# A two-layer float32 decoder step on one core: decode's retention update split in two and moved partly into the out and gate phases, Strassen over all 16 K tiles in the heads

## The chip, the core and the metric

The kernel runs on one core of a Trainium2 chip. The metric is the device time of one execution in microseconds (us); a kernel is timed several times and the median counts. Beside the times there is the profile of one execution, taken by the hardware profiler. TensorE (PE in the profile) multiplies matrices, VectorE (DVE) and ScalarE (ACT) work element by element on 128 partitions, GpSimd (POOL) here mostly issues transfers, and SyncE (SP) issues the loads of weights.

## What is computed

One inference step of a decoder trunk with two layers, for a prompt of 512 positions and 8 sample rows (one new token each), all in float32. The model width is 2048. Per layer:

```
h = rmsnorm(x, norm_g)
z = h @ w_in                      # 2048 x 8192: b, c, xc, g_conv (1024 each) and q, k, v, g_ret (4 heads of 256)
y_conv = b * conv3(c * xc) * silu(g_conv)
q, k = rope(q), rope(k) / 16
# retention, per head with decay gamma_h:
#   prompt: o_n = sum over m <= n of gamma^(n-m) (q_n . k_m) v_m, in chunks; the final state is an output
#   sample: S_new = gamma * S + k v^T ;  o = q . S_new ;  S_new is an output
y_ret = groupnorm(o) * gn_g * silu(g_ret)
x = x + concat(y_conv, y_ret) @ w_out
x = x + sigmoid(x @ w_pg) * (p[i] @ w_ple)
```

After both layers a final rmsnorm follows. The sample part of the retention is called decode below: 4 heads x 8 rows = 32 states of 256 x 256 numbers per layer, 256 KB each, that are read from DRAM, decayed, increased by an outer product, reduced against the query and written back.

## The kernel before

**Tiling.** Activations are kept transposed: a K tile is 128 model columns (partitions) by 520 columns, the 512 prompt positions and the 8 sample rows. A weight matrix has 16 K tiles, and output tiles of 128 columns are made in pairs (`pair`, line 396). Every float32 product is made of three float32r matmuls on high and low parts (`mm3`, lines 247 to 249): hi x hi, hi x lo, lo x hi. The 520 columns are worked on as two halves of 260, so each matmul has 260 columns. Weights come by SP into a ring `raw` of 32 tiles of 128 columns; `split_w` (lines 229 and 230) makes the high part on ScalarE and the low part on VectorE, into a ring of 60 such tiles that TensorE reads.

**Strassen.** `strassen` (line 290) handles the first s of the 16 K tiles of a pair as a 2 x 2 block product, with the K tiles in two groups, the two output tiles and the two column halves. It makes 7 products instead of 8, each over s/2 tiles. For that it adds and subtracts weight blocks on VectorE (`add`, line 319; four times s/2 tiles) and uses sums of operands prepared once per stage (`operand_sums`, lines 413 to 416, split by lines 551 and 552). The K tiles from s to 15 that are left over go through plain products afterwards, which need a fourth PSUM bank and one copy more. `plain` does a pair without Strassen. How many K tiles go through Strassen is written out by pair in the lists `HEADS`, `CONVS`, `OUT_ROWS` and `GATES` (0 means plain); the host packs the weights' K tiles in the order that each entry needs (`k_order`).

**Stages of a layer.** (1) The heads: for each of 4 heads four pairs make q, k, v and the gate; rope, then the parts are stored to DRAM (`hs`), and nine later steps per head do the prompt's chunked retention. (2) The convolutions: two pairs for each of 8 column tiles. (3) The out phase: 8 pairs with w_out, plus the residual (line 1139), stored as `x1s`. (4) The gate phase: 8 pairs with w_pg, the sigmoid and the embedding product, stored as `x2s`. The last layer ends with a tail of its own in place of the last gate pair. In layer 0 the first two pairs of the heads are done in a preamble.

**Decode before.** `sample_load` (lines 769 and 770) loads a state and, by a broadcast to 128 partitions, its key and query from DRAM (`kq`). `sample_step` scales the state by gamma on ScalarE (line 776), adds key times value on VectorE (line 780, twice 256 columns), stores the state (line 781) and reduces it against the query on VectorE (line 784, twice, each a main instruction and a short one that reads the accumulator). `sample` does one step and one load; it is called after each head pair and in the middle of every second one, and once or twice per column tile of the convolutions. At the last column tile, what is left is finished and `sample_norm` normalises the sums (matmuls of line 1371 against a constant).

**Order of the work.** The Tile framework orders each engine's instructions by priority and by a simulation of its own; `keep` holds marked instructions in program order among themselves. Two lists of callbacks interleave side work: `middle` is emptied after the fifth of a Strassen pair's seven products (or at half of a plain pair), and one entry of `later` is run after the fourth product and one at the end of each pair (in a plain pair right after `middle`, and at its end). Small loads and stores all go through GpSimd's queue (`SIDE`), in order. Tiles live in 75 slots, given out in the order in which they came free; operands of the next stage are built ahead (`fill`) only when enough slots are free.

## Times and profile before

| | |
|---|---|
| device time, median of 3 runs | 2169.59 us (2166.01 to 2169.92) |
| the profiled execution, first to last instruction | 2167.3 us (no other time is given for it) |
| TensorE matmuls | 17861 records, busy 99% of the span |
| VectorE, ScalarE, GpSimd busy | 87%, 58%, 20% |
| mean granted TensorE clock | 0.999 of full speed |
| DMA | 387 MB, mean 179 GB/s |

The median lies 2.3 us above the profiled span. Stages in the profiled execution, by the lines that run: layer 0 heads and convolutions to about 725 us, out phase to about 897, gate phase to about 1105; layer 1 heads and convolutions to about 1790, out phase to about 1970, gate phase and tail to the end. How to read the rows: "L230 DVE" is line 230 of the kernel on VectorE; "out<-in" are the program's own names; "x1031" is a count; after the bar stand busy us, the mean ns of one instruction, and the engine's idle time just before, with what ended it. Matmuls overlap, so a busy TensorE can still be short of matmuls: their number in a stretch tells.

### The profile page before, as it was taken

The numbers are of one execution on the slowest core, as the hardware profiler recorded it, in microseconds if no ns is written. First come the engines' busy times: TensorE is split into PE (matmuls) and PEld (weight loads), VectorE is DVE, ScalarE is ACT, GpSimd is POOL, SyncE is SP. The second block draws the span as 40 slices with busy tenths as digits, with TensorE's granted clock in tenths as the row PEclk, the third lists the DMA queues.
The fourth block names the chain that finished last, engine by engine and source line by source line (L and its number), as shares of the span: only waits on it lengthen the run. The fifth ranks groups of instructions, "written<-read, shape, count | busy, mean of one in ns | idle before, by whom it ended". The sixth has DMA issues, their size and how long they took to land. (4 is left out here: it accounts for less than half of the span.)

```text
span 2167.3 us, 48178 instructions
## 1 busy us (share of the span) xinstructions
PE 2147.8 (99%) x17861; PEld 2142.1 (99%) x17861; DVE 1896.1 (87%) x3849; ACT 1264.5 (58%) x2647; POOL 430.6 (20%) x746
## 2 busy tenths in 40 slices
PE   9999999999999999999999999999999999999998
PEld 9999999999999999999999999999999999999998
DVE  8889988998999987987997988989999998879884
ACT  8656655565555655655765655565645555456565
POOL 2313222211001211200212222231111022011011
PEclk9999999999999999999999999999999999999999
DMA  8555565545543745645645566664464355566455
GB/s 288 171 175 197 181 217 184 178 157 175 158 129 118 238 156 187 215 154 160 215 144 175 172 213 191 189 209 170 151 182 149 120 158 202 176 207 200 128 164 198
DMA packets 182861, 387.31 MB, mean 179 GB/s; under 512 B 25888, under 2 KB 56352, under 8 KB 182624
## 3 DMA queue, kind: packets, MB, share of 16 engines
q1 hardware_dynamic: 128704, 212.98, 31.6%
q0 software_dynamic: 53056, 169.84, 23.8%
q8 instruction: 140, 2.29, 0.4%
q10 hardware_dynamic: 864, 1.39, 0.2%
q14 instruction: 97, 0.79, 0.1%
HBM read 318.96 MB, written 65.15 MB: 177 GB/s over the span
## 5 line engine op out<-in xcount | busy, mean ns | idle before, releaser
L247 PE MATMUL ps_g<-slot,split 128*128 128x260 f32 x5465 | 1531.6, 284 | 7.2 <-ACT slot L307 2.9
L248 PE MATMUL ps_g<-slot,split 128*128 128x260 f32 x5465 | 1534.3, 282 | 0.3 <-DVE slot L555 0.3
L249 PE MATMUL ps_g<-slot,split 128*128 128x260 f32 x5461 | 1519.9, 283 | 0.5 <-DVE split L230 0.5
L229 ACT ACTIVATE split<-raw 128x512 fp32r<-128x512 f32 (+2 forms) x1347 | 777.3, 596 | 583.1 <-DVE raw L319 213.2
L247 PEld LDWEIGHTS ps_g<-slot,split 128*128 128x128 f32 x5465 | 1024.0, 188 | 10.1 <-ACT slot L307 3.7
L248 PEld LDWEIGHTS ps_g<-slot,split 128*128 128x128 f32 x5465 | 1028.5, 188 | 0.5 <-DVE slot L555 0.5
L249 PEld LDWEIGHTS ps_g<-slot,split 128*128 128x128 f32 x5461 | 1019.8, 188 | 1.0 <-DVE split L230 1.0
L230 DVE TENSOR_TENSOR split<-raw,split 128x512 fp32r<-128x512 f32 (+2 forms) x1346 | 849.2, 652 | 172.5 <-PE ps_g L248 85.4
L319 DVE TENSOR_TENSOR raw<-raw 128x512 f32<-128x512 f32 (+1 forms) x660 | 428.9, 660 | 32.5 <-DMA raw<-wi 23.7
L307 ACT ACTIVATE slot<-ps_g 128x260 f32<-128x260 f32 x336 | 127.4, 381 | 140.6 <-PE ps_g L249 122.7
L551 ACT ACTIVATE slot<-slot 128x520 fp32r<-128x520 f32 (+1 forms) x212 | 109.2, 562 | 46.6 <-DVE slot L414 11.1
L552 DVE TENSOR_TENSOR slot<-slot,slot 128x520 fp32r<-128x520 f32 (+1 forms) x212 | 124.4, 620 | 4.1 <-ACT slot L551 3.9
L781 POOL DMA_DIRECT2D o_rets<-slot x64 | 35.3, 552 | 351.6 <-DVE slot L780 131.7
L307 DVE TENSOR_TENSOR slot<-ps_g,slot 128x260 f32<-128x260 f32 x168 | 70.9, 424 | 6.0 <-PE ps_g L249 3.7
L869 POOL DMA_DIRECT2D slot<-hs x64 | 46.2, 724 | 118.7 <-DVE split L230 42.7
L814 POOL DMA_DIRECT2D hs<-slot x64 | 35.6, 556 | 139.3 <-DVE slot L755 61.3
L780 DVE SCALAR_TENSOR_TENSOR slot<-slot,vs,slot 128x256 f32<-128x256 f32 x128 | 56.1, 481 | 4.5 <-ACT slot L776 4.3
L746 DVE TENSOR_TENSOR slot<-slot,slot 128x520 f32<-128x520 f32 x80 | 55.8, 698 | 4.7 <-DMA o_rets<-slot 3.7
L770 POOL DMA_DIRECT2D slot<-sret x64 | 35.5, 554 | 114.6 <-ACT split L229 37.3
L1058 POOL DMA_DIRECT2D slot<-x1s x76 | 40.8, 538 | 87.6 <-PE ps_g L249 27.2
L1209 POOL DMA_DIRECT2D x2s<-slot x30 | 16.4, 545 | 201.6 <-DVE slot L1204 200.6
L771 POOL DMA_DIRECT2D slot<-kq x64 | 34.9, 547 | 106.0 <-DVE slot L876 22.2
(217 smaller groups left out, 1733.8 us busy)
## 6 DMA issues: line engine op xcount, KB each, us to landing
raw<-wi SPq DMA_DIRECT2D x377, 256.0 KB, 3.9
raw<-wo SPq DMA_DIRECT2D x128, 256.0 KB, 5.4
raw<-wg SPq DMA_DIRECT2D x122, 256.0 KB, 4.1
raw<-wi SPq DMA_DIRECT2D x136, 192.0 KB, 4.0
slot<-x1s POOLq DMA_DIRECT2D x76, 260.0 KB, 5.1
slot<-sret POOLq DMA_DIRECT2D x64, 256.0 KB, 4.0
hs<-slot POOLq DMA_DIRECT2D x64, 256.0 KB, 4.0
slot<-hs POOLq DMA_DIRECT2D x64, 256.0 KB, 5.2
```

The costliest lines, as they stand in the source:

```text
L229: S.activation(hi, raw, AF.Copy)
L230: V.tensor_tensor(lo, raw, F(hi), SUB)
L247: PE.matmul(out, wh, xh, start=start, stop=False, skip_group_check=more)
L248: PE.matmul(out, wh, xl, start=False, stop=False, skip_group_check=more)
L249: PE.matmul(out, wl, xh, start=False, stop=stop, skip_group_check=more)
L307: fn(*args)
L319: V.tensor_tensor(out[:, n], x[:, n], y[:, n], op)
L551: keep(S.activation(hi, src[:, n], AF.Copy))
L552: V.tensor_tensor(lo, src[:, n], F(hi), SUB)
L746: V.tensor_tensor(out[:, n], v, table[:, n], MUL)
L780: keep(V.scalar_tensor_tensor(st[:, c], k, vs[:, h, e, b : b + 1], st[:, c], MUL, ADD))
L869: SIDE.dma_start(t[:, :512].rearrange("p (m n) -> p m n", m=2), src)
```

## The change

The lists ask for 16 K tiles where they asked for 14, in the heads and in the first two convolution pairs (the last convolution pair stays at 14). Decode is taken apart. In the heads and convolutions, each state is loaded and reduced against the query with gamma as the factor, without the new key and value; the part of the new key and value in the output, gamma * (q . k/gamma) * v, is worked out for all states at once in `sample_norm` (two matmuls with ones, four small VectorE operations). The queries of two rows come in one broadcast load. The states themselves are updated in the out and gate phases by a chain of three callbacks, each one `update` call apart: `key_load` broadcasts the key, `state_add` makes key times value/gamma on ScalarE and adds the old state to it by an accumulating load from DRAM, `state_out` scales by gamma on ScalarE and stores. One call of `update` does one step of each of three states. It is called in the middle of each out and gate pair, after each, and once more in every second out pair. The vector with gamma is replaced by immediate numbers.

```diff
-HEADS = [[0, 0, 0, 8] + [14] * 12, [0] + [14] * 15]
-CONVS = [[14] * 2 + [16] * 13 + [14]] * 2
+GAMMA = [1.0 - 2.0 ** (-5 - h) for h in range(H)]
+HEADS = [[0, 0, 0, 8] + [16] * 12, [0] + [16] * 15]
+CONVS = [[16] * 15 + [14]] * 2
...
         def sample_load(h, b):
-            st, kb = get(), get()
+            st = get()
             SIDE.dma_start(st[:, :512], sret[l, h, b])
-            SIDE.dma_start(kb[:, :512], kq[l, h, b].rearrange("c d -> (c d)").partition_broadcast(P))
-            return h, b, st, kb
-
-        def sample_step(h, b, st, kb):
-
-            keep(S.activation(st[:, :512], st[:, :512], AF.Identity, scale=gam(h)))
-            k = kb[:, 256:512]
+            if b % 2 == 0:
+                queries.append(get())
+                src = kq[l, h, b : b + 2, :2].rearrange("b c d -> b (c d)").partition_broadcast(P)
+                SIDE.dma_start(queries[-1][:, :512].rearrange("p (b c) -> p b c", b=2), src)
+            return h, b, st, queries[-1]
+
+        def sample_step(h, b, st, q):
+
             for e in range(2):
                 c = slice(256 * e, 256 * e + 256)
-                keep(V.scalar_tensor_tensor(st[:, c], k, vs[:, h, e, b : b + 1], st[:, c], MUL, ADD))
-            SIDE.dma_start(o_rets[l, h, b], st[:, :512])
-            for e in range(2):
-                c = slice(256 * e, 256 * e + 256)
-                V.tensor_tensor_reduce(k, st[:, c], kb[:, :256], 1.0, 0.0, MUL, ADD, osum[:, e, h, b : b + 1])
-            put(st, kb)
+                n = slice(256 * (b % 2), 256 * (b % 2) + 256)
+                keep(V.tensor_tensor_reduce(st[:, c], st[:, c], q[:, n], GAMMA[h], 0.0, MUL, ADD, osum[:, e, h, b : b + 1]))
+            put(st)
+            if b % 2:
+                put(q)
...
+        def key_load(h, b):
+            st = get()
+            SIDE.dma_start(st[:, 256:512], kq[l, h, b, 2:].rearrange("c d -> (c d)").partition_broadcast(P))
+            return h, b, st
+
+        def state_add(h, b, st):
+            for e in range(2):
+                c = slice(256 * e, 256 * e + 256)
+                keep(S.activation(st[:, c], st[:, 256:512], AF.Copy, scale=vs[:, h, e, b : b + 1]))
+            SIDE.dma_start(st[:, :512], sret[l, h, b], accum_op=ADD)
+            return h, b, st
+
+        def state_out(h, b, st):
+            keep(S.activation(st[:, :512], st[:, :512], AF.Copy, scale=GAMMA[h]))
+            SIDE.dma_start(o_rets[l, h, b], st[:, :512])
+            put(st)
+
+        keyed, added = [], []
+
+        def update():
+
+            if added:
+                state_out(*added.pop(0))
+            if keyed:
+                added.append(state_add(*keyed.pop(0)))
+            if states:
+                keyed.append(key_load(*states.pop(0)))
+
+        states = [(h, b) for h in range(H) for b in range(NS)]
...
+            V.scalar_tensor_tensor(qk[:, :, h], qks[:, :2, :NS], GAMMA[h], qks[:, 2:, :NS], MUL, MUL)
...
-                V.scalar_tensor_tensor(vs[:, h, e, :], t[:, SEQ:T], 1.0 / 16, rb[:, SEQ:T], MUL, MUL)
+                V.scalar_tensor_tensor(vs[:, h, e, :], t[:, SEQ:T], 1.0 / 16 / GAMMA[h], rb[:, SEQ:T], MUL, MUL)
...
             Gt.ready = m // 2
             middle.append(lambda: O.fill(MORE_OUT, 0))
+            middle.append(update)
+            if m % 4:
+                later.append(update)
             zs = pair(O, wo[l], m, m // 2, Gt)
+            update()
...
             middle.append(lambda: Gt.fill(MORE_GATE, 0))
+            middle.append(update)
...
             Gt.fill(MORE_GATE, 0)
+            update()
             Gt.need(m // 2 + 1)
...
+    ps = pr.tile([P, 512], F32, tag="r", name="ps_qk")
+    for d in range(2):
+        PE.matmul(ps[:, :n], ones, qk[:, d].rearrange("p h b -> p (h b)"), start=d == 0, stop=d == 1)
+    own = small.tile([P, 2, H, NS], F32, tag="sq", name="own", bufs=1)
+    for e in range(2):
+        V.tensor_tensor(own[:, e], vs[:, :, e], ps[:, :n].rearrange("p (h b) -> p h b", b=NS), MUL)
+        V.tensor_tensor(osum[:, e], osum[:, e], own[:, e], ADD)
```

14 lines of the change are left out of this document (7 added, 7 removed).

## The prediction

> **What bounds the kernel now.** I read the page first, then who TensorE waits for, then the engines' busy time in stretches cut where one stage gives way to the next.
>
> ```profile
> span 2167.3 us, 48178 instructions
> PE 2147.8 (99%) x17861; PEld 2142.1 (99%) x17861; DVE 1896.1 (87%) x3849; ACT 1264.5 (58%) x2647; POOL 430.6 (20%) x746
> ```
>
> ```profile
> PE ps_g L247 <- ACT slot L307: 2.9, 4, 1.3
> PE ps_g L247 <- ACT ps_g L307: 1.6, 2, 1.2
> PE ps_g L247 <- ACT split L229: 1.5, 2, 1.3
> ```
>
> The second fence is the list of waits of TensorE, longest first (us in total, times, longest). Nobody holds TensorE for more than 3 us in 2167. The next view gives us and instructions per engine in a stretch, in the order PE, weight loads, DVE, ACT, POOL, then granted clock, DMA share and GB/s.
>
> ```profile
> 300.00:350.00 50.00, 50.00 (x420) 50.00 (x419) 47.27 (x104) 27.83 (x62) 14.01 (x26) 1.00 0.65 210
> 700.00:735.00 35.00, 31.68 (x260) 31.07 (x260) 35.00 (x75) 26.51 (x71) 10.66 (x20) 1.00 0.80 268
> 735.00:830.00 95.00, 95.00 (x794) 94.98 (x793) 79.59 (x141) 47.49 (x93) 14.04 (x27) 1.00 0.51 162
> 830.00:890.00 60.00, 60.00 (x503) 60.00 (x502) 49.37 (x92) 35.79 (x72) 14.39 (x27) 1.00 0.71 234
> 890.00:915.00 25.00, 25.00 (x211) 25.00 (x210) 24.80 (x54) 13.81 (x26) 4.86 (x9) 1.00 0.57 184
> 1105.00:1480.00 375.00, 373.93 (x3119) 372.74 (x3118) 331.45 (x725) 218.37 (x488) 94.79 (x164) 1.00 0.59 182
> 1770.00:1800.00 30.00, 28.15 (x233) 27.72 (x232) 29.66 (x65) 23.10 (x64) 10.14 (x19) 1.00 0.83 287
> 1965.00:1990.00 25.00, 25.00 (x211) 25.00 (x210) 24.72 (x51) 15.54 (x28) 4.63 (x9) 1.00 0.43 130
> ```
>
> A full stretch holds 420 matmuls in 50 us, 0.119 us each: TensorE is issue-bound there at full clock. Matmuls are missing only where a stage begins: 35 us should hold 294 and 700:735 has 260, so 34 x 0.119 = 4.0 us are lost; 1770:1800 should hold 252 and has 233, 2.3 us. In both (convolutions into out phase) VectorE is full. It is full too where out gives way to gate (890:915, 1965:1990), but there TensorE loses nothing: the split weights made ahead cover it. So the number of matmuls sets the time, and VectorE is the engine to break first.
>
> **Matmuls removed.** A Strassen pair over s K tiles takes 7 products x s/2 tiles x 3 matmuls, and 12 matmuls for each tile left over: s = 14 gives 147 + 24 = 171, s = 16 gives 168. The lists change 14 to 16 in 12 + 15 head pairs and in two convolution pairs of each layer: 31 pairs, 93 matmuls, 93 x 0.119 = 11.1 us. The Trainium skill ("TensorE: Matmul & The Clock Gate", section "Wait — 56ns, not 53.3ns?") puts a warm matmul at its columns over 2.4 GHz plus 2.5 ns, which for 260 columns is an estimated 110.8 ns and would make the saving 10.3 us; the trace's 119 ns disagrees, and I keep the trace's.
>
> **Weights of these pairs.** Rows by shape (busy us, mean ns, idle before):
>
> ```profile
> L230 DVE TENSOR_TENSOR split<-raw,split 128x512 fp32r<-128x512 f32 x1031 | 695.0, 690 | 147.8 <-PE ps_g L248 81.2 <-ACT split L229 51.8 <-issue 6.1
> L319 DVE TENSOR_TENSOR raw<-raw 128x512 f32<-128x512 f32 x520 | 354.1, 688 | 17.6 <-DMA raw<-wi 12.1 <-DMA raw<-wo 2.9
> L230 DVE TENSOR_TENSOR split<-raw,split 128x384 fp32r<-128x384 f32 x249 | 137.1, 555 | 16.2 <-ACT split L229 9.9 <-PE ps_g L248 3.4 <-ACT slot L551 1.9
> L319 DVE TENSOR_TENSOR raw<-raw 128x384 f32<-128x384 f32 x140 | 77.4, 554 | 14.9 <-DMA raw<-wi 11.6 <-DMA raw<-wg 2.8
> L230 DVE TENSOR_TENSOR split<-raw,split 128x256 fp32r<-128x256 f32 x66 | 27.3, 423 | 8.5 <-ACT split L229 7.6 <-PE ps_g L248 0.8
> L229 ACT ACTIVATE split<-raw 128x512 fp32r<-128x512 f32 x1032 | 632.3, 626 | 462.3 <-DVE raw L319 188.2 <-PE ps_g L249 166.4 <-PE ps_g L248 45.1
> L229 ACT ACTIVATE split<-raw 128x384 fp32r<-128x384 f32 x249 | 127.2, 518 | 84.0 <-DVE raw L319 25.0 <-PE ps_g L248 24.2 <-PE ps_g L249 17.9
> L229 ACT ACTIVATE split<-raw 128x256 fp32r<-128x256 f32 x66 | 27.3, 415 | 36.7 <-DMA raw<-wi 29.0 <-PE ps_g L248 5.2 <-PE ps_g L249 1.9
> L307 ACT ACTIVATE slot<-ps_g 128x260 f32<-128x260 f32 x336 | 127.4, 381 | 140.6 <-PE ps_g L249 122.7 <-DVE osum L784 4.6 <-DVE slot L746 4.3
> ```
>
> VectorE at s = 14: 7 x (0.555 + 0.690) + 4 x (0.554 + 0.688) + 2 x 0.423 = 14.53 us; at 16: 14 x 0.690 + 8 x 0.688 = 15.16. That is +0.63 a pair, +19.7 us over 31. ScalarE goes from 7 x (0.518 + 0.626) + 2 x 0.415 + 6 x 0.381 = 11.12 to 14 x 0.626 + 5 x 0.381 = 10.67, because with no tiles left over one copy falls away. Bytes are the same. The raw ring holds four blocks of eight tiles, as in the 13 convolution pairs already at 16.
>
> **Decode, in the heads.**
>
> ```profile
> L780 DVE SCALAR_TENSOR_TENSOR slot<-slot,vs,slot 128x256 f32<-128x256 f32 x128 | 56.1, 481 | 4.5 <-ACT slot L776 4.3
> L784 DVE CUSTOM_DVE_ANT_0 slot<-slot,slot 128x256 f32<-128x256 f32 x128 | 53.9, 421 | 0.0
> L776 ACT ACTIVATE slot<-slot,vec 128x512 f32<-128x512 f32 x64 | 45.7, 714 | 0.0
> L781 POOL DMA_DIRECT2D o_rets<-slot x64 | 35.3, 552 | 351.6 <-DVE slot L780 131.7 <-issue 81.3 <-ACT split L229 72.7
> ```
>
> Each of 64 states loses two 0.481 us instructions on VectorE (61.6 us in all) and 0.714 on ScalarE; the reductions of 784 stay and now wait for the state's load directly. The code takes three decode steps per two head pairs, so VectorE gains 1.5 x 0.962 = 1.44 a pair against +0.63: the heads (331.45 of 375 us busy) get lighter by 0.8 a pair, and the longer weights cost nothing. Were that cover gone, +0.63 would still fit in the 12% that VectorE idles. The two small operations per head on query and key are under a microsecond and off the path.
>
> **Decode, in the out and gate phases.** Each state now has a key broadcast (issue on POOL), two ScalarE products, an accumulating load, one ScalarE scaling and a store. Priced by the nearest rows:
>
> ```profile
> L1263 ACT ACTIVATE slot<-slot,vec 128x256 f32<-128x256 f32 x16 | 7.5, 498 | 2.5 <-DMA slot<-x2s 1.6 <-DVE slot L1275 1.0
> slot<-sret POOLq DMA_DIRECT2D x64, 256.0 KB, 4.0
> slot<-x1s POOLq DMA_DIRECT2D x76, 260.0 KB, 5.1
> o_rets<-slot POOLq DMA_DIRECT2D x64, 256.0 KB, 3.1
> ```
>
> ScalarE: 64 x (2 x 0.498 + 0.626) = 104 us over some 630 us in which 735:830 shows it half busy: it stays under three quarters. POOL: 3 x 64 x 0.552 = 106 us on a queue at 15%. Queued behind each POOL issue that waits for ScalarE are the residual loads, the x1 and x2 stores and the next operands' loads. DMA: 640 KB x 64 = 42 MB in 630 us, 65 GB/s on top of 162; 830:890 runs at 234 with TensorE full, so I price it at nothing.
>
> No accumulating load is in the trace. It is at least a plain load (4.0 us; a gain is excluded, since it is added work) and at most a load of this stage and then a store, 5.1 + 3.1 = 8.2. I take 5.1, the same queue, bytes and stage. The next update scales the same state, so ScalarE, which is in order, waits if the landing is late, with the weight splits behind it. Updates stand one after the fifth of seven products, one after the pair, and in four out pairs of each layer one after the fourth: distances of 48 matmuls (5.7 us) and 120 (14.3), and 24 (2.9) in those pairs. At 5.1 only the last is too short, by 2.2 us a pair; VectorE idles (95 - 79.59)/95 = 16% there, 3.2 us per 20 us pair, which hides it. In the last out pair, a plain one, two updates stand back to back: ScalarE may wait the whole 5.1 us just where VectorE is full (24.80 of 25), and three slots fewer are free for the gate's operands. What was made ahead covers most of it: I take 1.0 us per layer between 0 and 5.1, **2.0 us**.
>
> **Own value sums at the end of the convolutions.**
>
> ```profile
> 664.68 0.53 PE L1371 MATMUL ps_sm<-osum,onesd 128*128 128x32 f32 x4
> 665.04 0.36 PE L247 MATMUL ps_g<-slot,split 128*128 128x260 f32 x1
> ```
>
> Two more matmuls of this kind are four records, 665.04 - 664.68 plus the longer first successor (0.08) = 0.44 us a layer, **0.9 us**. The four small VectorE operations lengthen a chain whose result the out phase reads; the last convolution pair, 171 x 0.119 = 20 us, lies between and hides them.
>
> **Sum.** -11.1 + 0.9 + 2.0 = -8.2 us. Against the profiled span of 2167.3 that is 2159.1; the median of the three runs, 2169.59, lies 2.3 above that span, and I carry this over: **2161.4 us**. A measurement of this kernel can tell about 0.2% (4.3 us) from no change.
>
> **Rivals.** *Slower: the accumulating load holds ScalarE* (8%). Place: the scaling of each state. In the out phase two pairs have three short distances, and two pairs' slack of 6.5 us covers (x - 2.9) + 2(x - 5.7) up to x = 6.9. At x = 8.2 it is 10.3 - 6.5 = 3.8 us for each of 8 such couples of pairs, 30 us: -8.2 + 30 gives 2191. It beats the saving from x = 7.3. For it: nothing in the trace bounds this transfer better. Against it: both plain ends land in 3 to 5 us. The Trainium skill ("DMA: Bandwidth & Descriptors", "Rules for kernel authors") says that an accumulating DMA reads its destination and writes it later, which speaks for the long end; no trace here shows one.
>
> *Slower: weights come late* (4%). If the added 65 GB/s lengthened the weight loads by more than the 3.2 us of slack per pair, each further microsecond would cost some 30 us; one microsecond gives 2191. 830:890 speaks against.
>
> *No change: the boundaries take it back* (16%). Both back-to-back updates cost their whole 5.1 us: -11.1 + 0.9 + 10.2 = 0.0, 2169.6. For it: VectorE at 24.80 and 24.72 of 25. Against: TensorE full there now.
>
> *More: VectorE's relief ends the starved stage starts* (10%). 4.0 + 2.3 us come back and the new updates cost nothing: -11.1 + 0.9 - 6.3 = -16.5, 2153.1. Against it: by the code it is the building of the out phase's operands that falls into these stretches, and the diff leaves that alone.
>
> The forecast has 62%. Should a list not take effect, the matmul count would tell; I give that no chance, since the lists are read in the loops themselves.
>
> **Range and chances.** 2155 to 2171: it takes in the boundary term at 0 and at its full 10.2 and leaves out the two slow cases (12%) and most of the large gain. Faster by over 0.2%: 0.62 + 0.10 = 0.72; within: 0.16; slower: 0.12.
>
> **What would show it.** TensorE's count falls by 93 and rises by 8 records, to 17776. The rows of 780 and 776 are gone. Right: the accumulating load lands within 6 us, ScalarE's waits on it are a few us in all, TensorE stays full between the boundaries. Wrong: matmuls per 50 us below 415 inside the out or gate phase, VectorE idle there for ScalarE, or new losses beyond 4 us at 890 or 1965.

## The result and the profile after

The changed kernel takes **2241.99 us** (median of 4 runs, 2236.36 to 2245.91) against 2169.66 for the kernel before (4 runs): a ratio of **1.0337, 95% interval [1.0319, 1.0354]**. It is slower by 72 us, where 8 us less was predicted. The page of the kernel after begins like this (span; then busy time, share of the span and instructions of each engine):

```profile
span 2244.1 us, 47798 instructions
PE 2161.9 (96%) x17776; PEld 2150.9 (96%) x17776; DVE 1885.2 (84%) x3675; ACT 1305.8 (58%) x2682; POOL 509.8 (23%) x842
```

TensorE has the 17776 records that were predicted, yet it is no longer full: 99% busy has become 96%. The waits of TensorE in the kernel after (us in total, times, longest) name who held it:

```profile
PE ps_g L248 <- ACT slot L1234: 36.1, 2, 18.5
PE ps_g L248 <- DVE slot L308: 8.8, 6, 2.9
```

Before, nobody held it for more than 3 us in total. Now two waits on a sigmoid (line 1234 of the kernel after) last 18 us each. To see in which stage the time goes, both traces are cut where the first matmul of a stage starts: heads with convolutions, out phase, gate phase, and the same for the second layer, whose gate phase holds the end of the kernel (so cut, the first gate phase of the kernel before ends at 1082.8 us, earlier than the 1105 given with its profile above). The columns are the stretch, its length, then busy us and instructions of PE, weight loads, DVE, ACT and POOL, the granted clock, the DMA share and GB/s. First the kernel before:

```profile
5.10:722.00 716.90, 713.31 (x5935) 711.77 (x5936) 649.45 (x1359) 429.98 (x915) 157.31 (x267) 1.00 0.57 181
722.00:893.10 171.10, 168.98 (x1407) 168.55 (x1406) 144.85 (x267) 93.95 (x193) 31.79 (x60) 1.00 0.62 202
893.10:1082.80 189.70, 189.70 (x1587) 189.70 (x1586) 163.48 (x315) 117.35 (x225) 26.98 (x51) 1.00 0.54 171
1082.80:1791.90 709.10, 706.31 (x5886) 704.08 (x5885) 641.00 (x1355) 412.77 (x893) 150.29 (x247) 1.00 0.55 172
1791.90:1961.30 169.40, 168.84 (x1407) 168.61 (x1406) 140.94 (x253) 92.31 (x184) 31.25 (x59) 1.00 0.60 197
1961.30:2167.30 206.00, 196.87 (x1636) 195.92 (x1634) 156.01 (x306) 115.84 (x240) 28.65 (x52) 0.99 0.51 166
```

And the kernel after, cut at the same six places of the program:

```profile
5.20:717.20 712.00, 708.59 (x5897) 707.19 (x5898) 640.57 (x1268) 412.54 (x835) 128.35 (x214) 1.00 0.52 165
717.20:907.40 190.20, 177.77 (x1406) 175.94 (x1405) 141.99 (x268) 110.72 (x242) 68.82 (x114) 0.96 0.78 233
907.40:1121.60 214.20, 194.39 (x1586) 192.95 (x1585) 163.95 (x314) 136.14 (x273) 58.12 (x98) 0.95 0.68 206
1121.60:1822.50 700.90, 699.69 (x5840) 698.21 (x5839) 636.70 (x1258) 397.16 (x808) 122.07 (x194) 1.00 0.49 155
1822.50:2009.90 187.40, 175.71 (x1407) 173.58 (x1406) 145.40 (x269) 111.78 (x236) 68.74 (x115) 0.97 0.80 239
2009.90:2244.10 234.20, 202.37 (x1636) 199.82 (x1634) 156.13 (x303) 135.12 (x289) 59.19 (x98) 0.94 0.63 190
```

In the first gate phase of before TensorE is never idle: 189.70 us for 1587 matmuls, 0.1195 us each. What a stage takes beyond its matmuls times 0.1195 us is **lost**. In the heads and convolutions the two layers take 712.0 + 700.9 = 1412.9 us instead of 1426.0: 13.1 us won. The out phases grow by 19.1 and 18.0 us, the gate phases by 24.5 and 28.2, with the same matmuls: 89.8 us given away. The difference, 76.7 us, is that of the two spans (76.8) but for the first cut, which lies 0.1 us later. It is more than the 72 us of the medians because the profiled execution of the kernel after was the longest of its four. So the saving came, and the stages to which the update was moved ate it seven times over.

The finer windows answer to those of the prediction:

```profile
300.00:350.00 50.00, 50.00 (x421) 50.00 (x420) 47.32 (x97) 26.06 (x53) 13.03 (x23) 1.00 0.55 171
850.00:900.00 50.00, 45.48 (x350) 44.85 (x350) 34.34 (x66) 29.03 (x61) 20.76 (x35) 0.93 0.89 269
900.00:950.00 50.00, 34.27 (x280) 33.45 (x278) 34.90 (x69) 26.55 (x54) 15.75 (x26) 0.89 0.70 209
```

The heads hold 421 matmuls in 50 us; the out phase holds 350 and its end 280. No engine is full there: VectorE does 34 of 50 us, ScalarE 29. The busiest are the DMA engines, with a share of 0.89 in 850:900; whether the traffic costs the time is asked below. Engines that are all partly idle mean that each waits for another, or for a transfer. The rows of the new instructions by line (busy us, mean ns, idle of the engine before them and what ended it) and then the answer for the accumulating load's line say for whom:

```profile
L803 ACT ACTIVATE slot<-slot,vs 128x256 f32<-128x256 f32 x128 | 63.5, 496 | 0.4
L808 ACT ACTIVATE slot<-slot 128x512 f32<-128x512 f32 x64 | 40.1, 626 | 93.6 <-DMA slot<-sret 93.5
L804 POOL DMA_DIRECT2D slot<-sret x64 | 56.7, 886 | 39.3 <-ACT slot L803 25.2 <-ACT slot L308 7.8 <-ACT split L230 2.2
L809 POOL DMA_DIRECT2D o_rets<-slot x64 | 35.1, 548 | 251.3 <-ACT slot L808 245.5 <-ACT slot L803 4.2 <-DMA slot<-x1s 1.3
L797 POOL DMA_DIRECT2D slot<-kq x64 | 36.9, 582 | 67.8 <-DMA o_rets<-slot 46.0 <-DVE slot L416 7.9 <-DMA x1s<-slot 7.5
```

```profile
L804 POOL DMA_DIRECT2D slot<-sret x64: 849/880/922, 730.7 to 2199.7; - x64
  ACT slot L808: 93.5, 34
DMA to landing us min/median/max: 3.8/5.6/10.0
```

ScalarE stands 93.5 us, in 34 of 64 updates, before the scaling (808), for the landing of the accumulating load. GpSimd stands 245.5 us before the store (809), for that scaling, with the loads of operands behind it in its queue; and the next key load (797) stands 46.0 us for the landing of an earlier store, whose slot it was given. The busy time of the new instructions was priced well (0.496 and 0.626 us, where 0.498 and 0.626 were predicted); the waits between them were not. ScalarE's timeline at the end of the first out phase shows one wait after the other (start, us, instruction, in brackets its idle time before):

```profile
924.05 0.63 ACT L808 ACTIVATE slot<-slot 128x512 f32<-128x512 f32 x1 [4.28 <-DMA slot<-sret]
924.59 1.03 ACT L803 ACTIVATE slot<-slot,vs 128x256 f32<-128x256 f32 x2
929.85 0.63 ACT L808 ACTIVATE slot<-slot 128x512 f32<-128x512 f32 x1 [1.27 <-DMA slot<-sret]
935.77 0.63 ACT L808 ACTIVATE slot<-slot 128x512 f32<-128x512 f32 x1 [2.79 <-DMA slot<-sret]
941.64 0.63 ACT L808 ACTIVATE slot<-slot 128x512 f32<-128x512 f32 x1 [1.79 <-DMA slot<-sret]
950.94 1.17 ACT L552 ACTIVATE slot<-slot 128x520 fp32r<-128x520 f32 x2 [3.36 <-DVE slot L415]
953.42 1.23 ACT L1234 ACTIVATE slot<-ps_g 128x260 f32<-128x260 f32 x4
```

Four scalings are (941.64 - 924.05)/3 = 5.9 us apart. That is one round: scaling, the next state's products, the issue of its accumulating load, its landing, its scaling. Each update needs the one before it: on ScalarE its products stand behind the scaling of the one before, and on GpSimd its load stands behind that one's store. Every second out pair holds three updates: at 5.9 us each these are 17.6 us of a pair of 20. At the change from out to gate five stand together. The sigmoid that should have freed four PSUM banks runs at 953.42. Between the last of these scalings and the sigmoid ScalarE splits operands of the gate phase and waits for VectorE to make their sums (3.36 us in the line before the sigmoid); VectorE in its turn had waited (1.74 us at 943.04) for a load that GpSimd issued behind a store. TensorE does almost nothing meanwhile:

```profile
915.00:935.00 20.00, 18.87 (x153) 18.25 (x152) 8.51 (x16) 8.78 (x18) 5.37 (x8) 1.00 0.61 157
935.00:954.00 19.00, 0.54 (x5) 0.34 (x3) 14.06 (x26) 10.40 (x20) 4.47 (x7) 0.61 0.41 98
939.20:959.70 20.50, 5.84 (x27) 5.84 (x28) 15.77 (x32) 10.96 (x21) 5.22 (x9) 0.50 0.45 116
```

### The profile page after: what moved, and what is told of

The parts are those of the page before. It is cut to its first block, busy times and chain, and to the rows that moved or that the text cites. A ratio compares the mean times of both kernels' runs of the same rounds, so it can differ in the third digit from the quotient of the medians.

```text
span 2244.1 us, 47798 instructions
## 1 busy us (share of the span) xinstructions
PE 2161.9 (96%) x17776; PEld 2150.9 (96%) x17776; DVE 1885.2 (84%) x3675; ACT 1305.8 (58%) x2682; POOL 509.8 (23%) x842
## 4 chain that ended last, share of the span: by engine, by line
PE 75%; DMA 10%; issue 6%; DVE 3%; ACT 3%; POOL 2%; SPq 0%; DVEq 0%; POOLq 0%; ACTq 0%
PE ps_g L248 23%; PE ps_g L250 23%; PE ps_g L249 23%; DMA slot<-sret 4%; DMA raw<-wo 1%; DVE split L231 1%; DMA raw<-wg 1%; DMA slot<-x1s 1%; ACT split L230 1%; ACT slot L803 1%; DVE raw L320 1%; DVE slot L553 0%; POOL slot L804 0%; DMA x2s<-slot 0%; POOL slot L1087 0%
## 5 line engine op out<-in xcount | busy, mean ns | idle before, releaser
L230 ACT ACTIVATE split<-raw 128x512 fp32r<-128x512 f32 (+1 forms) x1285 | 782.5, 623 | 504.8 <-DVE raw L320 278.3
L231 DVE TENSOR_TENSOR split<-raw,split 128x512 fp32r<-128x512 f32 (+1 forms) x1284 | 860.0, 686 | 233.4 <-PE ps_g L249 123.8
L320 DVE TENSOR_TENSOR raw<-raw 128x512 f32<-128x512 f32 (+1 forms) x660 | 444.2, 685 | 37.9 <-DMA raw<-wo 18.1
L769 POOL DMA_DIRECT2D slot<-sret x64 | 35.9, 560 | 277.4 <-ACT split L230 104.1
L808 ACT ACTIVATE slot<-slot 128x512 f32<-128x512 f32 x64 | 40.1, 626 | 93.6 <-DMA slot<-sret 93.5
L809 POOL DMA_DIRECT2D o_rets<-slot x64 | 35.1, 548 | 251.3 <-ACT slot L808 245.5
L804 POOL DMA_DIRECT2D slot<-sret x64 | 56.7, 886 | 39.3 <-ACT slot L803 25.2
L803 ACT ACTIVATE slot<-slot,vs 128x256 f32<-128x256 f32 x128 | 63.5, 496 | 0.4
L1141 POOL DMA_DIRECT2D yc<-slot x16 | 8.9, 554 | 202.9 <-DVE slot L745 202.9
```

Of the source, the lines that this page charges most:

```text
L230: S.activation(hi, raw, AF.Copy)
L231: V.tensor_tensor(lo, raw, F(hi), SUB)
L320: V.tensor_tensor(out[:, n], x[:, n], y[:, n], op)
L803: keep(S.activation(st[:, c], st[:, 256:512], AF.Copy, scale=vs[:, h, e, b : b + 1]))
L804: SIDE.dma_start(st[:, :512], sret[l, h, b], accum_op=ADD)
```

## The experiments

Each was run beside the kernel before. The table gives the time, the ratio with its interval, and the us lost in both layers' heads with convolutions, out phases and gate phases, worked out as above (0.1195 us per matmul, the trace cut at the same places of the program; since some matmul records are missing from a trace, a figure is good to about 1 us).

| kernel | us | ratio [95%] | heads | out | gate |
|---|---|---|---|---|---|
| before | 2169.66 | 1 | 14 | 5 | 11 |
| after | 2241.99 | 1.0337 [1.0319, 1.0354] | 11 | 42 | 64 |
| e1 lists only | 2182.41 | 1.0062 [1.0049, 1.0075] | 36 | 8 | 11 |
| e2 decode only | 2247.38 | 1.0364 [1.0348, 1.0380] | 9 | 36 | 63 |
| e8 no update | 2164.99 | 0.9981 [0.9972, 0.9991] | 9 | 15 | 10 |
| e4 plain load | 2215.38 | 1.0214 [1.0200, 1.0228] | 10 | 30 | 50 |
| e5 no scaling | 2216.76 | 1.0218 [1.0204, 1.0232] | 9 | 34 | 45 |
| e6 two more slots | 2253.38 | 1.0384 [1.0369, 1.0400] | 45 | 25 | 56 |
| e7 e6, out one later | 2224.60 | 1.0249 [1.0231, 1.0267] | 39 | 11 | 46 |
| e9 boundary free | 2217.66 | 1.0224 [1.0208, 1.0239] | 10 | 51 | 26 |
| e10 later and moved | 2208.06 | 1.0192 [1.0168, 1.0216] | 23 | 28 | 29 |
| e11 update last | 2253.87 | 1.0395 [1.0380, 1.0410] | 11 | 44 | 65 |
| e12 store from ScalarE | 2254.03 | 1.0395 [1.0380, 1.0409] | 8 | 41 | 77 |
| e13 e10 and e12 | 2223.63 | 1.0262 [1.0247, 1.0276] | 25 | 40 | 35 |
| e14 sigmoid first | 2242.72 | 1.0349 [1.0334, 1.0365] | 11 | 39 | 61 |
| e15 twelve moved | 2195.78 | 1.0136 [1.0121, 1.0151] | 25 | 16 | 25 |
| e16 sixteen moved | 2178.41 | 1.0054 [1.0037, 1.0070] | 15 | 17 | 22 |
| e18 e16, norm early | 2175.79 | 1.0028 [1.0011, 1.0046] | 15 | 10 | 22 |
| e19 e8, norm early | 2150.17 | 0.9916 [0.9902, 0.9930] | 8 | 6 | 11 |
| e20 spread out | 2197.57 | 1.0126 [1.0109, 1.0144] | 30 | 28 | 14 |

The theory after the result was: the update's scaling waits for its landing, the wait stands on two in-order queues, and the updates are too close together. The rivals: the lists cost it, the added traffic costs it, or it is one place in the program's order.

### Which half of the change: e1, e2, e8

e1 is the kernel before with the new lists alone:

```
-HEADS = [[0, 0, 0, 8] + [14] * 12, [0] + [14] * 15]
-CONVS = [[14] * 2 + [16] * 13 + [14]] * 2
+HEADS = [[0, 0, 0, 8] + [16] * 12, [0] + [16] * 15]
+CONVS = [[16] * 15 + [14]] * 2
```

> The kernel before with only the lists at 16; decode stays where it was. Theory A (the loss is ScalarE waiting, in order, for the accumulating load that the taken-apart decode adds in the out and gate phases): nothing of that is here, so the time falls by the 93 matmuls, 11.1 us, to about 2158, give or take 4, with VectorE's +19.7 us of weights hidden in the heads. Rival B (VectorE could not carry 16 K tiles in the heads with decode beside it, so the two parts need each other): TensorE shows waits in the heads and the time stays at 2170 or rises.

e2 is the kernel after with the old lists (the same diff the other way round).

> The changed kernel with the lists back at 14. Theory A: the whole loss of some 90 us in the out and gate phases stays, and only the 11.1 us of matmuls come back on top: about 2253 (2245 to 2262), with ScalarE's scaling again waiting some 90 us for the accumulating load. Rival C (the two parts collide, for instance in slots or in the scheduler's order): the time falls clearly below the changed kernel's 2242.

e8 is the kernel after without any call of `update`, so that the new sample states are not written:

```
-            middle.append(update)
-            if m % 4:
-                later.append(update)
             zs = pair(O, wo[l], m, m // 2, Gt)
-            update()
...
-            middle.append(update)
...
-            update()
```

> The changed kernel without any update call: the new states of the sample rows are neither made nor stored; all other outputs are. Every theory that puts the loss into the chain of updates expects the out and gate phases as in the kernel before and the heads' gain kept: 2153 to 2160. If the own value sums in sample_norm or the order of the heads cost something of their own, it stays above 2165.

The lists alone are **slower** by 0.6%. The windows of e1's heads and convolutions show why:

```profile
5.20:727.40 722.20, 711.70 (x5894) 708.56 (x5895) 658.53 (x1331) 423.88 (x871) 157.24 (x266) 1.00 0.56 180
1090.80:1805.30 714.50, 703.97 (x5833) 699.87 (x5834) 652.95 (x1318) 408.14 (x842) 150.62 (x247) 1.00 0.54 169
```

There are fewer matmuls than before, yet both stretches are longer than before's 716.9 and 709.1. VectorE is busy 91%, and still TensorE waits: 91% as a mean over 700 us holds shorter stretches that are full. From 250 to 255 us, for example, VectorE is busy throughout, and TensorE makes 33 matmuls there and 15 in the next 5 us, where a full 5 us hold 44. The lists pay only together with VectorE's relief. e2 keeps nearly the whole loss, so the lists aren't its cause. e8 takes it away: the two out and gate phases lose 25 us instead of 106 (before: 16), with the same stage cuts:

```profile
715.70:891.30 175.60, 171.85 (x1407) 171.21 (x1406) 143.97 (x272) 93.61 (x198) 36.37 (x65) 0.98 0.59 196
891.30:1081.30 190.00, 189.80 (x1586) 189.59 (x1585) 163.33 (x315) 117.28 (x225) 27.36 (x52) 1.00 0.53 173
```

So some 81 us belong to the 64 updates. e8 is also a ceiling, and a low one: only 0.2% faster than before, and above the 2153 to 2160 us that were expected. Its gate phase is as good as before's; its out phase lasts 4.5 us longer than before's 171.1. That remainder is taken up below (e18, e19).

### What in the update: e4, e5

e4 loads the state plainly over the products, so the new states lack the key times value; e5 leaves the scaling out, so they lack the decay:

```
-            SIDE.dma_start(st[:, :512], sret[l, h, b], accum_op=ADD)
+            SIDE.dma_start(st[:, :512], sret[l, h, b])
```

> The changed kernel with a plain load in place of the accumulating one; the outer product of key and value is overwritten, so the new states lack it. All waits, slots, bytes and the order of the program stand as they were. Theory A1 (what costs is that the scaling stands right behind a load on ScalarE, whatever the load): the landing falls from a median of 5.6 us to 4 or 5, and the time by less than a third of the loss, to 2215 or more. Rival A2 (the accumulation itself is slow, it reads and writes): landing near 3.7 us as in the heads, ScalarE's waits under 30 us, time near 2175.

```
-            keep(S.activation(st[:, :512], st[:, :512], AF.Copy, scale=GAMMA[h]))
```

> The changed kernel without the last scaling on ScalarE; the new states lack the factor gamma. The accumulating load, its bytes, the slots and the store stay; the wait for the landing now stands in GpSimd's queue, ahead of the other small transfers. Theory A: ScalarE waits for no landing, the 18 us stalls ahead of the first sigmoids go, and most of the 90 us come back: 2160 to 2185. Rival D (the loss is the added traffic, the slots or the queue on GpSimd): the time stays above 2220.

Each takes back about a third, 27 and 25 us. In e4 the load lands after 2.8/4.7/8.8 us (least, median, most) and its issue takes 538 ns, where the accumulating one took 3.8/5.6/10.0 us and 880 ns in the same place: 0.9 us less of each landing and 0.3 of each issue. In e5 ScalarE has no scaling to wait with, and the same wait turns up on GpSimd (waits of POOL, from the first out phase to the end of the first gate phase):

```profile
POOL o_rets L808 <- DMA slot<-sret: 69.5, 31, 6.2
POOL slot L797 <- DMA o_rets<-slot: 56.0, 14, 7.2
```

The store now waits for the landing itself, and the next key load for the store's landing. So neither the kind of load nor ScalarE's wait is the cause by itself: the round stays, and whoever comes next in it waits. The theory had forecast 2160 to 2185 us for e5 and was wrong there.

### Distance and place: e6, e7, e9, e10

e6 gives two more slots, paid for with eight split buffers, as the control for e7; e7 then scales and stores two calls behind the accumulating load instead of one:

```
-NSLOT = 75
+NSLOT = 77
-SPLIT = 60
+SPLIT = 52
```

> The changed kernel with 77 slots for 75 and a split ring of 52 tiles for 60 (the room comes from there). Theory S (the three-step chain has too few slots: a key load is given the slot that the store of the state before has just left, and waits in GpSimd's queue for that store to land, with the operand loads behind it): those 25 us of waits per layer mostly go and the time falls by 15 us or more, below 2227. Rival (slots are not it): 2236 to 2250, or a little more for the shorter ring.

```
-            if added:
+            while len(added) > 1 or (added and not keyed and not states):
                 state_out(*added.pop(0))
```

> As the run with two more slots, and the scaling and store of a state come two calls of update after its accumulating load in place of one. Theory L (ScalarE and then GpSimd's queue stand because the landing is awaited one call later, often only two or three instructions of ScalarE later): ScalarE's waits for the landing fall from 93 us to under 15, GpSimd's for the scaling fall too, the two 18 us stalls ahead of the first sigmoids shrink, and the time falls to 2165 to 2195. Rival D (traffic or the number of transfers in GpSimd's queue): within 15 us of the run with two more slots.

e9 keeps the one call of distance but holds the last out pair and the first gate pair free of updates:

```
-            middle.append(update)
-            if m % 4:
-                later.append(update)
+            if m < KT - 2:
+                middle.append(update)
+                later.extend([update] * (2 if m == 0 else 1))
...
-            update()
+            if m < KT - 2:
+                update()
...
+            if m:
                 middle.append(update)
...
+            if m:
                 update()
```

> The changed kernel with the same number of updates, but none in the last out pair and in the first gate pair of a layer, where all of the gate's operands are built; they are made up for by one more call in each of the other out pairs. Theory P (the place: five updates inside 34 us there hold ScalarE and GpSimd's queue, so that the first sigmoid, and with it all five PSUM banks, comes 18 us late, and TensorE then runs at half clock for some 20 us): both 18 us stalls go with their half clock, about 50 us: 2185 to 2205. Rival (a late landing costs as much anywhere): 2225 to 2250, the loss moves into the out pairs.

e10 has both edits (76 slots, 58 split buffers):

> Two earlier edits together: the scaling and store stand two calls behind the accumulating load instead of one, and the last out pair and the first gate pair hold no update (the other out pairs take them over); one more slot, paid for with two split buffers (58) instead of the eight of the earlier run. Theory (too short a distance and a wrong place are two separate costs): they add. From 2242, the place gave 24 and the distance 29 between the two runs with 77 slots, and two split buffers fewer cost the heads some 5 (eight cost 34 over both layers): about 2194. Rival (both edits cure the same wait, so the second finds nothing left): not under 2210. Rival (the added traffic itself sets the out and gate phases): about 2215, as with one edit alone.

e6's two slots take 25 us from the out and gate phases, and its shorter split ring costs the heads 34: slots help, and the ring can't pay for them. From e6 to e7 the distance brings 29 us, 14 in the out and 10 in the gate phases; ScalarE's waits for the landing fall from 93.5 us to 20.3. The theories had asked for more of e6, e7 and e9 (under 2227, 2165 to 2195, 2185 to 2205): each names a part of the cost and none the whole. e9 moves the loss more than it removes it: the gate phases lose 38 us less and the out phases, which took the updates over, 9 more; the time falls by 24. Together (e10) the out and gate phases lose 56 us instead of 106. The theory had them add to 2194, the rival to not under 2210; with 2208.06, at the rival's edge, they add in part, and the shorter ring takes 12 us of the gain in the heads. Traffic as the sole cause is out: e10 moves the same bytes through the same stages as the kernel after.

### Order and queues: e11, e12, e13, e14

e11 writes the update behind each pair's residual adds or sigmoids instead of ahead of them:

```
             zs = pair(O, wo[l], m, m // 2, Gt)
-            update()
...
                     x1[m + i] = x
+            update()
...
             Gt.fill(MORE_GATE, 0)
-            update()
             Gt.need(m // 2 + 1)
...
                     x2[m + i] = x
+            update()
```

> The changed kernel with one move: the update that stands behind each out and gate pair is written behind that pair's residual adds or sigmoids instead of ahead of them; nothing else moves. Theory (ScalarE is in order, so a sigmoid written behind a scaling that waits for its landing keeps four PSUM banks): the two stalls of 18 us at the start of the gate phases fall below 6 us each and the half clock behind them goes too, 20 to 40 us in all: 2202 to 2222. Rival (the stall comes of the operands, not of the order on ScalarE): the stalls stay above 12 us and the time lies within 2236 to 2246.

e12 issues the store from ScalarE; e13 is e10 with the same line:

```
-            SIDE.dma_start(o_rets[l, h, b], st[:, :512])
+            S.dma_start(o_rets[l, h, b], st[:, :512])
```

> The changed kernel with one move: the store of the new state is issued by ScalarE, right behind the scaling, instead of by GpSimd. Theory (GpSimd's queue stands for ScalarE and the loads of operands behind it come late): GpSimd no longer waits for line 808 (245 us), loads land earlier, the out and gate phases win 15 to 25 us: 2217 to 2227. Rival (ScalarE's own wait for the landing is the whole cost, and the queue is off the path): within 0.3% of 2242, or some us above it for 64 issues on ScalarE.

> The first of these four kernels with the store of the new state issued by ScalarE as well. Theory (distance, place and GpSimd's queue are three costs that add): 10 to 20 us below the first, 2175 to 2185, near the kernel before. Rival (with two calls between landing and scaling, the queue no longer waits long): within 0.3% of the first.

e14 writes the sigmoids ahead of `Gt.fill`, `update` and `Gt.need`:

```
-            Gt.fill(MORE_GATE, 0)
-            update()
-            Gt.need(m // 2 + 1)
             for i, z in enumerate(zs):
...
                     x2[m + i] = x
+            Gt.fill(MORE_GATE, 0)
+            update()
+            Gt.need(m // 2 + 1)
```

> The changed kernel with the gate phase's sigmoids and residual adds written ahead of the building of the next operands and of the update behind the pair, instead of behind them. Theory (at the first gate pair four PSUM banks wait for a sigmoid that stands on ScalarE behind operands whose loads come late): the two stalls of 18 us and most of the 20 us of half clock behind each go: 2195 to 2215. Rival (the operands themselves are late, and TensorE would only wait for them one pair on): the stalls turn up as waits on operand splits, 2235 to 2250.

All four theories fell. e11 leaves the stalls (17.0 us the longest) and is slower. In e12 GpSimd no longer waits for the scaling, and waits for the products of the next state in its stead (waits of POOL, 717 to 1121 us):

```profile
POOL slot L804 <- ACT slot L803: 65.9, 16, 10.4
POOL slot L804 <- ACT slot L308: 46.7, 9, 8.5
```

The products stand on ScalarE behind the scaling that waits for its landing: the round again, one station on. A wait on GpSimd also isn't a loss by itself: in the kernel before it stood 102.7 us before the stores of `x2s` and 93.3 before those of `x1s` in the same two phases (722 to 1083 us), with TensorE all but full. e14 is the clearest. Its longest wait of TensorE is 5.2 us, so the 18 us stalls are gone, and it is not faster. The gate phase in three stretches, first of the kernel after:

```profile
915.00:974.00 59.00, 39.42 (x301) 38.59 (x300) 33.57 (x62) 29.67 (x58) 13.98 (x22) 0.83 0.57 153
974.00:994.00 20.00, 20.00 (x169) 20.00 (x168) 16.73 (x32) 13.23 (x28) 5.58 (x9) 1.00 0.53 162
1021.00:1121.00 100.00, 99.77 (x827) 99.16 (x827) 82.66 (x163) 71.04 (x144) 28.60 (x49) 1.00 0.74 232
```

and of e14:

```profile
915.00:974.00 59.00, 49.30 (x384) 47.56 (x383) 40.73 (x78) 33.31 (x66) 14.39 (x24) 0.94 0.59 151
974.00:994.00 20.00, 17.66 (x135) 17.45 (x134) 14.25 (x26) 11.51 (x24) 4.97 (x8) 0.91 0.69 218
1021.00:1121.00 100.00, 93.18 (x774) 92.54 (x773) 77.24 (x154) 68.77 (x138) 29.05 (x50) 0.99 0.75 232
```

The banks come free early and TensorE does 83 matmuls more in the first stretch. It gives them back, 34 in the second and 53 in the third, where the kernel after had lost nothing: both gate phases lose 61 us in e14, against 64. The largest wait of the list was a symptom: taken away, the loss turned up in other places.

### How many, how close: e15, e16

Both keep a part of the states on VectorE in the heads, as before (`MOVED` of each head's 8 states go the new way), and call `update` once per pair, in its middle, not in the first gate pair; e16 adds a second call behind the first four out pairs:

```
+MOVED = 3
...
+                if b >= MOVED:
+                    keep(V.scalar_tensor_tensor(st[:, c], q[:, 256:512], vs[:, h, e, b : b + 1], st[:, c], MUL, ADD))
...
-        states = [(h, b) for h in range(H) for b in range(NS)]
+        states = [(h, b) for h in range(H) for b in range(MOVED)]
...
             middle.append(update)
-            if m % 4:
-                later.append(update)
             zs = pair(O, wo[l], m, m // 2, Gt)
-            update()
...
+            if m:
                 middle.append(update)
```

> A mixture: of the 32 states of a layer 12 are updated in the out and gate phases as in the changed kernel, one call per pair, in the middle of it, none in the first gate pair; the other 20 are updated in the heads on VectorE as in the kernel before; lists at 16. Theory (the loss comes of several updates standing close together, each one a round trip of 6 us that the next waits for; alone in a pair of 20 us it is covered): out and gate phases lose under 10 us in all, and the heads keep a part of the 13 us: 2158 to 2175. Rival (each update costs its share of the 90 us wherever it stands, 1.4 us): 24 updates cost 34 us, the heads gain at most 13: 2190 or more.

> The same mixture with 16 of 32 states moved: the first four out pairs hold a second update at their end, one product or two behind the middle one. Theory of packing: four short distances a layer cost at most one landing of 5.6 us each, part of it covered: 2160 to 2190. Rival (a price of 1.4 us for each update): 32 updates, 45 us less 13: 2200 or more.

The out and gate phase of e16's first layer (4 states of each head moved):

```profile
719.30:896.30 177.00, 170.88 (x1406) 168.99 (x1405) 142.54 (x263) 105.08 (x228) 50.72 (x89) 1.00 0.74 225
896.30:1095.60 199.30, 192.98 (x1587) 191.54 (x1585) 162.21 (x317) 123.05 (x241) 40.43 (x72) 0.99 0.60 190
```

With those of the second layer they lose 38 us. Less the 25 that e8 loses without updates, 32 updates cost 14 us; e15's 24 cost 17; the 64 of the kernel after cost 81. Half the updates, set farther apart, cost a sixth, so there is no fixed price of each update (1.3 us would make 41 us here). The accumulating loads of e16 even land later, after 6.5 us in the median against 5.6, but ScalarE waits for them 9.8 us in all instead of 93.5, and in e15 not at all. The weights land as late as in the kernel after, too: in the first layer's out and gate phases a load of w_out landed in the median after 5.2 us in the kernel before, 6.0 in the kernel after and 6.1 in e16, one of w_pg after 4.1, 6.3 and 6.6. Both speak against the traffic as the cause.

That closeness is all of it isn't shown. e15 and e16 change number, distance and place together, and what is left doesn't sit where calls are close: e16's out phases, with four close couples in each layer, lose 2 us more than e8's, while its gate phases, with each call alone in its pair, lose 12 more (in e15: 1 and 15). So e15 missed both halves of its theory (under 10 us lost in the out and gate phases, 2158 to 2175 in all): these phases lose 41 us, and the heads, with 20 states of a layer on VectorE, 25. e16's time lies within its theory. Seen over e1, e15, e16 and the kernel after, with 32, 20, 16 and 0 states on VectorE, they lose 36, 25, 15 and 11.

### The start of the out phase: e18, e19

Without updates (e8) the out phase still began worse than before. GpSimd's timeline of e8 there:

```profile
709.21 1.07 POOL L1092 DMA_DIRECT2D slot<-ys  x2 [6.27 <-PE ps_g L250]
711.88 5.92 POOL L1419 TENSOR_TENSOR rsn<-va,half_neg 128x32 f32<-128x32 f32 x1
717.76 2.18 POOL L1092 DMA_DIRECT2D slot<-ys  x4
```

The power at the end of the small normalization chain takes 5.92 us, and the loads of the out phase's first operands queue behind it. In the kernel before it ran at 673.74 (5.84 us), 40 us ahead of the out phase. The framework's ordering by simulation (the planner, from here on) had moved the chain: its first mean stands at 697 us in e8, at 665 before. The edit gives it priority, in e16 (e18) and in e8 (e19):

```
-                sample_norm(nc, small, pr, osum, qk, vs, ones, onesd, half_neg, gs, lambda k: gn_g(l, k))
+                with tc.high_priority():
+                    sample_norm(nc, small, pr, osum, qk, vs, ones, onesd, half_neg, gs, lambda k: gn_g(l, k))
```

> The mixture with 16 of 32 states moved, and the chain that normalizes the retained values of the decode tokens (own sums, two means, a power on GpSimd of 5.8 us) given high priority, so that it runs as early as its data allow, as it did in the kernel before. Theory (the planner put this chain 30 us later than before, so that the power stands on GpSimd just where the loads of the out phase's operands are issued): the starts of the out phases win 4 to 5 us each: 2166 to 2172. Rival (the starts are short of VectorE, which builds operands, not of loads): 2174 to 2182.

> The kernel without any update in the out and gate phases (the new sample states are not written), with the same chain at high priority. Theory (the late power delays the out phase's operand loads): 2165 falls by 6 to 10 us, to 2155 to 2159, and this would be the most that the whole change could win. Rival: within 2162 to 2168.

In e19 the power starts at 661.22, and its out phases are:

```profile
715.90:884.50 168.60, 168.60 (x1407) 168.59 (x1406) 143.32 (x264) 92.37 (x192) 32.79 (x62) 1.00 0.63 205
1773.30:1946.60 173.30, 170.39 (x1406) 169.97 (x1405) 144.16 (x259) 92.42 (x184) 31.80 (x60) 0.99 0.62 200
```

The first is full from end to end; the second, against expectation, wins only 1.2 us. The median falls by 15 us, to 0.9916 of before, more than the 6 to 10 expected. The two profiled executions differ by 8.7 us (2161.0 and 2152.3), nearly all of it in the out phases; the other 6 us aren't accounted for. The time of e19 is what the whole change, with the chain early, could have brought with updates at no cost. In e18 the out phases lose 10 us instead of 17, but the medians differ by 2.6 us, with intervals that overlap, and the time lies in the rival's range: seen in the stage, not told by the time.

### A version made from this: e20

e20, made from e18, takes the updates out of the gate phase and puts 14 of a layer into the convolutions, two calls per pair from the seventh on; 8 stay on VectorE in the heads, 10 in the out phase:

```
-MOVED = 4
+MOVED = 6
...
+        rest = [states.pop() for _ in range(10)][::-1]
...
+            if 3 <= j < CJ - 1:
+                middle.append(update)
             zc, zx = pair(X, wi[l], mt, mt // 2 - skipped, O)
+            if 3 <= j < CJ - 1:
+                update()
...
-            if m:
-                middle.append(update)
```

> A version made from what the runs showed: per layer 8 of 32 states are updated in the heads on VectorE, 14 by accumulating load in the first convolution pairs from the seventh on (two calls per pair, 6 to 14 us apart), 10 in the out phase (one call in the middle of a pair, a second one behind the first four), none in the gate phase; the chain of the decode normalization has high priority. Sum of the losses by stage as earlier runs had them: heads 7 and 5, out 4.4 and 5.6, gate 0.6 and 11, 34 us against 31.5 in the kernel before, less 10.2 of matmuls: about 2161, if two calls per convolution pair cost nothing. Theory (the update is cheap where ScalarE and GpSimd have room and two calls are a landing apart): 2156 to 2166. Rival (in the convolutions VectorE is full, and ScalarE's waits on landings hold the weight splits there as they did in the out phase): 8 short distances a layer cost up to 5 us each, 2175 or more.

The time lies where the rival put it, and half of the rival's mechanism shows. The gate phases are nearly as before (14 us lost), and in the convolutions, from 560 to 720 us, ScalarE waits as it did in the out phase:

```profile
ACT slot L815 <- DMA slot<-sret: 20.1, 6, 5.0
```

TensorE makes 1097 matmuls from 560 to 700 us where e18 makes 1170. VectorE is not full there, though (116.94 of 140 us); ScalarE's waits for landings are what is new. That the out phases lose 28 us, though they hold as many calls as in e18 (10 us lost), isn't explained: the planner orders the whole program anew with every edit. No version that does the whole work beat the kernel before; e18 comes nearest, at 1.0028 [1.0011, 1.0046].

## Why the prediction was wrong, step by step

**Right:** the count (17776), 0.119 us a matmul and so 11.1 us; the small cost of the own sums on TensorE (the heads and convolutions won 13.1 us); the durations of the new instructions; the landing, taken as 5.1 and measured as 5.6 us in the median, inside its bounds. That the traffic costs nothing was not measured by itself, but e10 and e16 speak for it; the weights did land up to 2.2 us later, within the 3.2 us that the prediction gave them.

**The step that failed** is "At 5.1 only the last is too short, by 2.2 us a pair; VectorE idles [...] which hides it", with the 2.0 us for the boundary that came of it. It set the landing against the distance between two calls, counted in TensorE's matmuls, and let VectorE's slack absorb the rest. The loads behind GpSimd's issues were named there, and given no price. The runs show in its place a round of 5.9 us through two in-order queues, in which every update needs the one before; three in a pair take 17.6 of 20 us, five stand together at the boundary, and operands, slots and PSUM banks queue behind. VectorE's slack hid little of it: in the first layer's out and gate phases VectorE itself waited 27.5 us for ScalarE's split weights, against 2.9 before. The term was not 2 us but 81 (e8).

The slow rival had the place right, the scaling behind the accumulating load, and the price and the threshold wrong. It wanted landings above 7.3 us and gave 30 us; a median of 5.6 us was enough, since it too looked at ScalarE's wait alone. e4, e5 and e12 show that with this wait eased or gone the next station of the round waits.

**The heads.** That the relief covers the longer weights held. "Were that cover gone, +0.63 would still fit in the 12%" did not: e1 has the cover gone, and its heads lose 36 us instead of 14. **The chain at the end of the convolutions** was said to be hidden by the last pair. Its own length is; but the planner moved it by some 30 us, and its power then delayed the operands' loads: between e8 and e19 the first layer's out phase falls by 7.0 us, the second's by 1.2. **The rival that VectorE's relief ends the starved stage starts** comes true only in e19's first layer.

**What stays open.** The shares of distance, place, slots and late operands in the 81 us: they overlap (e10), and each edit lets the planner order the rest anew. What the added work itself costs, without its waits (103.6 us on ScalarE and 128.7 on GpSimd), was not tried alone, nor is it known why single updates cost more in the gate phase than couples in the out phase. Why e13 is slower than e10, and e20's out phases than e18's, wasn't settled. A round with three or more updates under way wasn't tried either; already the two slots of e6 cost the heads 34 us.

## What to carry to other kernels

Price a moved step as a round: follow one item through every queue it crosses to the point where the next item may start, and compare that time, times the items per stage, with the length of the stage. Room on each engine says nothing about it; in the stages that lost most no engine beside TensorE was over 78% busy (VectorE, 145.40 of 187.40 us). When one wait stands far above the others, ask what would be late next without it: taking away the 18 us stalls (e14), ScalarE's wait (e5) or GpSimd's (e12) brought nothing or a third, while half as many items, set farther apart (e16), took five sixths of the loss away. Which of the two, the number or the distance, did how much is open.

## What the runs showed of the hardware

An accumulating load of 256 KB landed after 3.8/5.6/10.0 us and took GpSimd 880 ns to issue, where the plain one in its place took 2.8/4.7/8.8 us and 538 ns (e4): 0.9 us and 0.34 us more. The kernel before has no such load.

The granted clock fell to half inside the 18 us stall: it is 0.50 from 939.20 to 959.70, beginning 4 us after the last matmul and ending 6 us after work resumed. In those 6 us 27 matmuls took 5.84 us, 0.216 each, so some 2.6 us are lost to it, a small addition to this stall. Over the whole kernel it is more. The clock is at 0.50 in ten stretches between 734 and 2062 us, 72 us together, in which TensorE is at work for 40.6 us. At 0.216 us for a matmul instead of 0.1195 that loses about 18 us; in e8, with 9.1 us of work in such stretches, about 4, and in the kernel before nothing between 20 and 2150 us. So by this estimate some 14 of the 81 us are the half clock that the waits bring with them. The Trainium skill ("TensorE: Matmul & The Clock Gate", "What's actually happening") says that the clock is halved after an idle window of about 3.4 us and released after a busy one; the 4 us here agree, the 6 us after the stall are somewhat longer. A shorter pause was enough in another place: the clock is at 0.50 from 881.2 us on, though TensorE's longest pause in the 15 us before was 1.8 us.
